# The order of matrix units in a Strassen MLP: one more unit of the first matmul ahead of a unit of the second, one fewer later

## The chip, the cores and the metric

The kernel runs on one NeuronCore of a Trainium2 chip. The metric is the device time of one execution in microseconds; the time given for a kernel is the median of several runs.

## The reference

Two decoder layers on 512 positions of width D = 1024, batch 1, in f32. Each layer modulates its norms with vectors from a condition `c`, mixes positions (layer 0 by pooling, layer 1 by a spatial gating unit), and then runs an MLP:

```python
for i in range(DEPTH):
    mod = c_act @ ada_w[i] + ada_b[i]
    sh1, sc1, g1, sh2, sc2, g2 = jnp.split(mod, 6, axis=-1)
    h = modulate(rmsnorm(x, norm_mix_g[i]), sh1, sc1)
    ...
    x = x + g1[:, None, :] * y
    h = modulate(rmsnorm(x, norm_mlp_g[i]), sh2, sc2)
    x = x + g2[:, None, :] * (jnp.square(jax.nn.relu(h @ mlp_w1[i])) @ mlp_w2[i])
return rmsnorm(x, final_g)
```

The MLP is 1024 to 4096 to 1024; it is most of the work, and the change concerns only it.

## The kernel before

**Precision.** TensorE has no full f32 product here: `split` (L170 to L178) writes a weight tile of 128 x 1024 as a rounded high part `wh` (ScalarE, L176) and a rest `wl` (VectorE, L177). `mm3` (L183 to L190) does every product as three matmuls: wl with the high part (L187), wh with the low part (L188), and wh with the high part (L190). The activations are cut likewise, `oh` on ScalarE (L638) and `ol` on VectorE (L639).

**Chunks and products.** `mlp` treats the 4096 hidden features in 4 chunks. M1 is the first matmul (into a chunk's hidden features), M2 the second (out of them). From chunk 1 on, M1 is done by the Strassen-Winograd scheme: each half (a or b) of a chunk is 7 products of block sums instead of 8. M2 of chunks 0 to 2 is done in the same way on the whole chunk. One product is a unit: an M1 unit (kind "s", written s1, s5, s6, ...) is 24 matmuls of 256 columns, an M2 unit (kind "p", written P1, P2, ...) 24 of 512. M1 of chunk c + 1 is interleaved with M2 of chunk c.

**Banks.** Products accumulate in PSUM where Winograd's sums allow: the M1 products 1, 6, 7, 4 pass through one bank of the tile `po` one after the other, 5 and 3 share another, and 2 has its own (`s_run`, L808ff). Between two products of one bank its content must be taken out: after 1, 6 and 5 by a ScalarE copy (L828), after 3 and 7 by a VectorE subtraction (L833, L835). After that come the squared ReLU's two ScalarE passes (L836, L667). M2's results are added into `y` by VectorE (L930), or copied by ScalarE (L933).

**Weights.** Some products need sums of weight blocks. These are built in place: by VectorE (L788), or by a DMA that accumulates into the tile, on GpSimd's queue. For M1 that is L783 on the tile `raw`: after the split of s6's weights, the block that makes s4's is added to them. For M2 it is L850 on the tile `bt` (from `w2`): P1's weights become P5's, these P6's, and these P4's, each as soon as the former has been split. Plain loads go over SyncE's queue.

**What sets the order.** The list `units` is written out by L975 to L988. PE runs it strictly as written. Ahead of each unit the loop at L1010 prepares further units (loads, weight sums, splits, cuts), at most 5 weight pairs ahead. On ScalarE, VectorE, GpSimd and SyncE the instructions are put in order by a scheduler when the kernel is built; at run time each engine works through its own queue in that order, so an instruction that waits holds up all behind it. The pools have 5 weight pairs `wh`/`wl`, 4 banks `po`, and 4 banks `pm` for M2.

The two tables of the changed line say how many M1 units come first (`lead`) and how many follow each M2 unit (`step`; M2's order is ORDER2 = 1, 2, 5, 6, 3, 7, 4). M1's order is ORDER = 1, 5, 6, 3, 7, 2, 4; the first half in layer 0's chunk 0 goes by ORDER2 with its 4 at the end. There, `early` is true. What is said below of "layer 0, chunk 0" is that of M2; its M1 units are those of chunk 1.

Of the kernel before, what the change touches and what calls it, by code (L numbers as in the profile page):

```python
# [81 lines left out]
def decoder_kernel(ctx: ExitStack, tc: tile.TileContext, xtok, vecs, rows, fgrow, ada0, adag, ada1, pool_w, w1s, w1, w1f, w1b, w2, w2e, w_v, w_u, w_o, wsT, lnp, bs, out):  # L82
# [561 lines left out]
    def mlp(i, first, extra, last, ending):  # L644
# [3 lines left out]
        with (  # L648
# [328 lines left out]
            for c in range(3):  # L977

                early = i == 0 and c == 0
                fs = [("s", (c + 1, j, m)) for j in range(2) for m in (ORDER2 if early and j == 0 else ORDER)]  # L980
                lead, step = (3, (0, 3, 2, 2, 2, 2, 0)) if early else (2, (1, 2, 3, 2, 2, 2, 0))
                units += fs[0:lead]
                fs = fs[lead:]
                for m, n in zip(ORDER2, step):
                    units.append(("p", (c, m)))
                    units += fs[0:n]
                    fs = fs[n:]
# [118 lines left out]
    ex += [(59, lambda: spread_cols(mods[0][:, c_g(1, 0) : c_g(1, 0) + KD], "gain0"))]  # L1106
    ex += [(n, modulation(q, get4)) for q, n in enumerate(COLUMNS) if q >= 19]
    mlp(0, first0, ex, gated, ending0)


# [6 lines left out]
    with (  # L1117
# [79 lines left out]
        for dh in range(2):  # L1197
            wo = blocks(w_o[dh])

            early = 6 if dh == 0 else KD  # L1200
# [60 lines left out]
    ex = [x for q in range(8) for x in modulation_late(48 + q, 8 + 5 * q, late_gb if q == 0 else get_gb)]  # L1261
    ex += [(58, lambda: spread_cols(mods[1][:, c_g(1, 0) : c_g(1, 0) + KD], "gain1"))]
    mlp(1, first1, ex, last1, lambda: None)


# [78 lines left out]
```

## Time and profile before

| | us |
|---|---|
| median of 3 runs | 855.63 (854.56 to 855.83) |
| the profiled execution | 853.81 |
| its span, first to last instruction | 852.1 |
| PE (TensorE) busy | 837.4 |
| DVE (VectorE) busy | 695.8 |
| ACT (ScalarE) busy | 490.9 |
| POOL (GpSimd) busy | 70.3 |

The mean granted clock of TensorE in the profiled execution is 0.993 of full speed. In the lines that follow, times in a timeline or in the chain of waits are microseconds from the start of the span. A row of a timeline has the start, the duration, the engine, the line, the operation, what it writes and reads, the count of equal operations in a row, and in brackets the idle time of the engine ahead of it with what ended it. Operations of one engine overlap a little in the profile, so what an operation costs its queue is read from one start to the next.

### The profile page before, as it was taken

The numbers are of one execution on the slowest core, as the hardware profiler recorded it, in microseconds if no ns is written. First come the engines' busy times: TensorE is split into PE (matmuls) and PEld (weight loads), VectorE is DVE, ScalarE is ACT, GpSimd is POOL, SyncE is SP. The second block draws the span as 40 slices with busy tenths as digits, with TensorE's granted clock in tenths as the row PEclk, the third lists the DMA queues.
The fourth block names the chain that finished last, engine by engine and source line by source line (L and its number), as shares of the span: only waits on it lengthen the run. The fifth ranks groups of instructions, "written<-read, shape, count | busy, mean of one in ns | idle before, by whom it ended". The sixth has DMA issues, their size and how long they took to land.

```text
span 852.1 us, 13021 instructions
## 1 busy us (share of the span) xinstructions
PE 837.4 (98%) x5068; PEld 744.6 (87%) x5068; DVE 695.8 (82%) x928; ACT 490.9 (58%) x728; POOL 70.3 (8%) x95
## 2 busy tenths in 40 slices
PE   9999999999999999999999999999999999999996
PEld 7778898998998998888888888999999999999885
DVE  6889798978997998867897865777788888987755
ACT  5286776765756567247233226666766666566521
POOL 3000011010101010000020001010101000111001
PEclk9999999999999999999999999999999999999998
DMA  8969998988888896724745636947888788777302
GB/s 349 418 234 323 357 216 217 288 212 236 211 282 195 274 237 205 272 98 173 256 166 176 218 123 224 320 94 202 208 238 221 207 222 241 182 168 243 125 25 99
DMA packets 44082, 186.53 MB, mean 219 GB/s; under 512 B 4955, under 2 KB 5107, under 8 KB 36726
## 3 DMA queue, kind: packets, MB, share of 16 engines
q1 hardware_dynamic: 35282, 137.72, 43.7%
q0 software_dynamic: 8304, 45.63, 26.7%
q10 hardware_dynamic: 436, 2.37, 0.8%
q8 instruction: 40, 0.66, 0.3%
q14 instruction: 20, 0.16, 0.1%
HBM read 179.39 MB, written 6.30 MB: 218 GB/s over the span
## 4 chain that ended last, share of the span: by engine, by line
PE 87%; DMA 6%; ACT 3%; DVE 2%; issue 1%; SPq 0%; POOLq 0%; POOL 0%; DVEq 0%; ACTq 0%
PE po L187 16%; PE po L188 16%; PE po L190 16%; PE pm L188 12%; PE pm L190 12%; PE pm L187 12%; DMA wh<-in_ada 2%; DMA bt<-in_w 2%; DMA wl<-in_ada 1%; DMA ada<-in_adag 1%; PE po L1182 1%; ACT sq L315 1%; PE px L1062 1%; ACT wh L176 0%; PE po L611 0%
## 5 line engine op out<-in xcount | busy, mean ns | idle before, releaser
L187 PE MATMUL po<-hb,wl 128*128 128x256 f32 (+2 forms) x633 | 187.9, 297 | 2.3 <-ACT g L828 2.1
L188 PE MATMUL po<-hb,wh 128*128 128x256 f32 (+1 forms) x632 | 187.2, 296 | 0.0
L190 PE MATMUL po<-hb,wh 128*128 128x256 f32 (+1 forms) x632 | 187.1, 296 | 0.0
L177 DVE TENSOR_TENSOR wl<-raw,wh 128x1024 fp32r<-128x1024 f32 (+1 forms) x128 | 152.8, 1198 | 39.4 <-ACT wh L176 36.8
L176 ACT ACTIVATE wh<-raw 128x1024 fp32r<-128x1024 f32 (+1 forms) x128 | 131.9, 1038 | 79.6 <-PE pm L190 26.7
L190 PE MATMUL pm<-wh,oh 128*128 128x512 f32 (+1 forms) x375 | 131.1, 367 | 0.0
L187 PE MATMUL pm<-wh,ol 128*128 128x512 f32 x336 | 131.0, 390 | 0.0
L188 PE MATMUL pm<-wl,oh 128*128 128x512 f32 x336 | 131.0, 390 | 0.0
L187 PEld LDWEIGHTS po<-hb,wl 128*128 128x128 f32 x633 | 119.6, 189 | 7.0 <-ACT g L828 2.3
L190 PEld LDWEIGHTS po<-hb,wh 128*128 128x128 f32 x632 | 119.5, 189 | 4.1
L188 PEld LDWEIGHTS po<-hb,wh 128*128 128x128 f32 x632 | 119.4, 189 | 3.9
L190 PEld LDWEIGHTS pm<-wh,oh 128*128 128x128 f32 x375 | 70.4, 188 | 14.7
L187 PE MATMUL po<-as,wl 128*128 128x256 f32 x288 | 79.9, 277 | 0.7 <-DVE wl L177 0.7
L188 PE MATMUL po<-as,wh 128*128 128x256 f32 x288 | 79.6, 277 | 0.0
L190 PE MATMUL po<-as,wh 128*128 128x256 f32 x288 | 79.6, 276 | 0.0
L177 DVE TENSOR_TENSOR wl<-bt,wh 128x1024 fp32r<-128x1024 f32 x48 | 58.4, 1222 | 23.5 <-ACT wh L176 23.5
L215 DVE SCALAR_TENSOR_TENSOR ada<-ada,cb 128x1024 f32<-128x1024 f32 x56 | 68.1, 1219 | 10.4 <-DMA ada<-in_ada 7.8
L187 PEld LDWEIGHTS pm<-wh,ol 128*128 128x128 f32 x336 | 63.1, 188 | 11.9
L188 PEld LDWEIGHTS pm<-wl,oh 128*128 128x128 f32 x336 | 63.1, 188 | 11.7
L176 ACT ACTIVATE wh<-bt 128x1024 fp32r<-128x1024 f32 x48 | 50.3, 1057 | 25.6 <-DMA bt<-in_w 15.9
L187 PEld LDWEIGHTS po<-as,wl 128*128 128x128 f32 x288 | 54.1, 188 | 0.9 <-ACT wh L176 0.9
L188 PEld LDWEIGHTS po<-as,wh 128*128 128x128 f32 x288 | 54.2, 188 | 0.0
(218 smaller groups left out, 1549.9 us busy)
## 6 DMA issues: line engine op xcount, KB each, us to landing
ada<-in_ada SPq DMA_DIRECT2D x72, 512.0 KB, 4.5
raw<-in_w1b SPq DMA_DIRECT2D x48, 512.0 KB, 5.5
b<-in_w SPq DMA_DIRECT2D x18, 1024.0 KB, 6.8
bt<-in_w POOLq DMA_DIRECT2D x18, 1024.0 KB, 8.0
raw<-in_w1b POOLq DMA_DIRECT2D x24, 512.0 KB, 5.7
raw<-in_w2e SPq DMA_DIRECT2D x16, 512.0 KB, 4.3
bt<-in_w SPq DMA_DIRECT2D x6, 1024.0 KB, 9.8
b<-in_w POOLq DMA_DIRECT2D x6, 1024.0 KB, 11.1
```

The source lines that it names most:

```text
L176: A.activation(h[:, c], r[:, c], AF.Copy)
L177: V.tensor_tensor(l[:, c], r[:, c], f32(h[:, c]), ALU.subtract)
L187: T.matmul(o[:, c], wl, mh[:, c], start=first and not c.start, stop=False, **kw)
L188: T.matmul(o, wh, ml, start=False, stop=False, **kw)
L190: T.matmul(o[:, c], wh, mh[:, c], start=False, stop=last and c.stop is None, **kw)
L215: V.scalar_tensor_tensor(r, r, 1.0, cb, ALU.mult, ALU.mult, accum_out=pmv[i, b][:, j : j + 1])
L315: A.activation(j, X(t)[:, c], AF.Square, scale=D**-0.5, accum_out=out)
L1062: T.transpose(px[:, 256 * q + P * r : 256 * q + P * r + P], xs[r][:, P * (k + q) : P * (k + q) + P], ident)
L1182: T.matmul(po[:, tok[t]], vt[t][:, ch, c0 : c0 + P], wb[:, 0, hd], start=True, stop=True)
```

## The change

```diff
                 fs = [("s", (c + 1, j, m)) for j in range(2) for m in (ORDER2 if early and j == 0 else ORDER)]
-                lead, step = (3, (0, 3, 2, 2, 2, 2, 0)) if early else (2, (1, 2, 3, 2, 2, 2, 0))
+                lead, step = (3, (0, 4, 2, 2, 2, 1, 0)) if early else (3, (1, 2, 2, 2, 2, 2, 0))
                 units += fs[0:lead]
                 fs = fs[lead:]
                 for m, n in zip(ORDER2, step):
                     units.append(("p", (c, m)))
                     units += fs[0:n]
                     fs = fs[n:]
```

In layer 0, chunk 0, four M1 units stand between P2 and P5 instead of three, and one instead of two between P7 and P4:

```
before  s1a s2a s5a P1 P2 s6a s3a s7a     P5 s4a s1b P6 s5b s6b P3 s3b s7b P7 s2b s4b P4
after   s1a s2a s5a P1 P2 s6a s3a s7a s4a P5 s1b s5b P6 s6b s3b P3 s7b s2b P7 s4b     P4
```

In the other five chunks three M1 units stand ahead of P1 instead of two, and two instead of three between P5 and P6:

```
before  s1a s5a     P1 s6a P2 s3a s7a P5 s2a s4a s1b P6 (the rest is equal)
after   s1a s5a s6a P1 s3a P2 s7a s2a P5 s4a s1b     P6
```

The amount of work of each kind is unchanged. Where instructions move, the queues show. PE first, at the end of s7a in layer 0, chunk 0 (`wh_1185` and `wl_1186` are s7a's weights, `wh_1228` is P5's first pair, `wh_1222` and `wl_1223` are s4a's in the changed kernel). Before:

```order
L188 MATMUL po_1045<-hb_96,wh_1185 128x256
L190 MATMUL po_1045<-hb_96,wh_1185 128x256
L187 MATMUL pm_1331<-wh_1228,ol_1225 128x512
L188 MATMUL pm_1331<-wl_1229,oh_1224 128x512
L190 MATMUL pm_1331<-wh_1228,oh_1224 128x512
```

After:

```order
L188 MATMUL po_1045<-hb_96,wh_1185 128x256
L190 MATMUL po_1045<-hb_96,wh_1185 128x256
L187 MATMUL po_1045<-hb_96,wl_1223 128x256
L188 MATMUL po_1045<-hb_96,wh_1222 128x256
L190 MATMUL po_1045<-hb_96,wh_1222 128x256
```

The bank `po_1045`, which s7a has just filled, is the bank of the next unit too; before, a unit of M2 with banks of its own stood between.

ACT at the same place, from the last split before P5's input cut on. `raw_955` and `raw_949` hold s3a's and s7a's weights, `oh_1224` (`oh_1255` after) is P5's input, `bt_1026` P5's weights, L828 takes s6a out of `po_1045`, `raw_941` is s4a's weights and `raw_1183` s1b's. Before:

```order
L176 ACTIVATE wh_1179<-raw_955 128x1024
L176 ACTIVATE wh_1185<-raw_949 128x1024
L638 ACTIVATE oh_1224<-s_1222 128x1024
L176 ACTIVATE wh_1228<-bt_1026 128x1024
L176 ACTIVATE wh_1232<-bt_1026 128x1024
L828 ACTIVATE g_1044<-po_1045 128x2x256
L176 ACTIVATE wh_1262<-raw_941 128x1024
L176 ACTIVATE wh_1295<-raw_1183 128x1024
```

After:

```order
L176 ACTIVATE wh_1179<-raw_955 128x1024
L176 ACTIVATE wh_1185<-raw_949 128x1024
L638 ACTIVATE oh_1255<-s_1253 128x1024
L176 ACTIVATE wh_1222<-raw_941 128x1024
L828 ACTIVATE g_1044<-po_1045 128x2x256
L176 ACTIVATE wh_1259<-bt_1026 128x1024
L176 ACTIVATE wh_1263<-bt_1026 128x1024
L176 ACTIVATE wh_1295<-raw_1183 128x1024
```

The split of s4a's weights has moved ahead of L828 and of P5's splits; P5's splits have moved behind L828.

DVE at the same place, from the low part of P5's input on; L835 takes s7a out of `po_1045`. Before:

```order
L639 TENSOR_TENSOR ol_1225<-s_1222,oh_1224 128x1024
L177 TENSOR_TENSOR wl_1229<-bt_1026,wh_1228 128x1024
L177 TENSOR_TENSOR wl_1233<-bt_1026,wh_1232 128x1024
L177 TENSOR_TENSOR wl_1263<-raw_941,wh_1262 128x1024
L833 TENSOR_TENSOR g_1044<-po_1116,g_1044 128x2x256
L177 TENSOR_TENSOR wl_1296<-raw_1183,wh_1295 128x1024
L215 SCALAR_TENSOR_TENSOR ada_1191,pmv_963<-ada_1191,cb_101 128x1024
L835 TENSOR_TENSOR g_1044<-g_1044,po_1045 128x2x256
```

After:

```order
L639 TENSOR_TENSOR ol_1256<-s_1253,oh_1255 128x1024
L177 TENSOR_TENSOR wl_1223<-raw_941,wh_1222 128x1024
L869 TENSOR_TENSOR s_1253<-s_1253,g_919 128x1024
L177 TENSOR_TENSOR wl_1260<-bt_1026,wh_1259 128x1024
L177 TENSOR_TENSOR wl_1264<-bt_1026,wh_1263 128x1024
L833 TENSOR_TENSOR g_1044<-po_1116,g_1044 128x2x256
L177 TENSOR_TENSOR wl_1296<-raw_1183,wh_1295 128x1024
L215 SCALAR_TENSOR_TENSOR ada_1191,pmv_963<-ada_1191,cb_101 128x1024
L835 TENSOR_TENSOR g_1044<-g_1044,po_1045 128x2x256
```

s4a's subtraction and L869 (a sum for P6's input, which stood behind L835) have moved ahead of P5's two subtractions; L835 is behind them all.

The last place is ACT at the head of layer 0, chunk 2. `raw_2312` holds the weights of s6a, `bt_2590` (`bt_2596` after) P1's, `oh_2672` (`oh_2703`) is the next M2 input, and L828 takes s1a out of `po_2612`. Before:

```order
L176 ACTIVATE wh_2596<-bt_2590 128x1024
L667 ACTIVATE g_2207<-g_2207 128x2x256
L176 ACTIVATE wh_2600<-bt_2590 128x1024
L638 ACTIVATE oh_2672<-g_2207 128x1024
L176 ACTIVATE wh_2606<-raw_2312 128x1024
L828 ACTIVATE g_2611<-po_2612 128x2x256
```

After:

```order
L667 ACTIVATE g_2207<-g_2207 128x2x256
L176 ACTIVATE wh_2564<-raw_2312 128x1024
L176 ACTIVATE wh_2602<-bt_2596 128x1024
L176 ACTIVATE wh_2606<-bt_2596 128x1024
L638 ACTIVATE oh_2703<-g_2207 128x1024
L828 ACTIVATE g_2611<-po_2612 128x2x256
```

The split of s6a's weights has moved ahead of P1's two.

## The prediction

> **What bounds the kernel now.** I read the page first, then the list of waits of PE, then the chain of waits in the stretch that the first wait lies in, and last the timelines of PE, ACT and DVE there. From the page:
>
> ```profile
> span 852.1 us, 13021 instructions
> PE 837.4 (98%) x5068; PEld 744.6 (87%) x5068; DVE 695.8 (82%) x928; ACT 490.9 (58%) x728; POOL 70.3 (8%) x95
> ```
>
> PE is busy 98% of the span, so only two things can move the time: idle gaps of PE, and stretches in which its granted clock is low. The diff changes no matmul, only their order. The list of PE's waits over the whole span has two that lie in the MLPs (the columns are the total, the count and the longest):
>
> ```profile
> PE po L187 <- ACT g L828: 2.1, 1, 2.1
> ...
> PE po L187 <- DVE wl L177: 0.9, 2, 0.7
> ```
>
> The first is the larger, and one wait. It lies in layer 0, chunk 0, ahead of product 7 of the first half of M1 (I write s7 for that unit, P5 for product 5 of M2). The chain of waits there:
>
> ```profile
> 111.65 15.97 DMA bt<-in_w
> 127.70 2.00 ACT wh L176 x2
> 129.71 0.49 ACT g L828
> ```
>
> The accumulating transfer that builds P5's weights took 15.97 us. ACT, which works in its queue's order, stood waiting for it, and behind the two splits stood the evacuation L828 of s6, whose bank s7 overwrites. PE's timeline and the windows cut at the 3.42 us steps in which the clock changes show what that cost:
>
> ```profile
> 127.87 0.28 PE L190 MATMUL po<-as,wh 128*128 128x256 f32 x1
> 130.25 0.38 PE L187 MATMUL po<-hb,wl 128*128 128x256 f32 x1 [2.10 <-ACT g L828]
> 134.69 0.39 PE L187 MATMUL pm<-wh,ol 128*128 128x512 f32 x1
> ...
> 127.11:130.53 3.42, 1.32 (x12) 1.12 (x11) 1.73 (x2) 2.49 (x3) 0.00 (x0) 1.00 1.05 280
> 130.53:133.95 3.42, 3.42 (x18) 3.42 (x18) 1.77 (x2) 1.85 (x2) 0.85 (x1) 0.50 1.03 322
> 134.69:140.15 5.46, 5.46 (x27) 4.55 (x26) 5.17 (x7) 2.27 (x4) 0.00 (x0) 1.00 0.99 260
> 140.15:142.89 2.74, 2.74 (x26) 2.74 (x25) 1.79 (x2) 2.74 (x5) 0.86 (x1) 1.00 0.82 211
> ```
>
> The columns of a window are its length, then busy time of PE, weight loads, DVE, ACT and POOL, the granted clock, the DMA share and GB/s. s7 should have begun at 127.98 (127.87 and a step of 0.11) and began at 130.25: 2.27 lost. PE was busy 1.32 of 3.42 us, and the next such window ran at clock 0.50. So s7 took 134.69 − 130.25 = 4.44 us, not the 2.74 of the undisturbed unit s4 (140.15 to 142.89): 1.70 more. P5 is the row of 5.46. Before, s7 and s4 stand with P5 between them, and the second half of M1 (s1b) starts at 142.89.
>
> **The change, term by term.** The new order puts s4 ahead of P5, and prepares it first. Two queues follow from that.
>
> *ACT.* Before, in order of time:
>
> ```profile
> 127.70 2.00 ACT L176 ACTIVATE wh<-bt 128x1024 fp32r<-128x1024 f32 x2 [5.00 <-DMA bt<-in_w]
> 129.62 0.58 ACT L828 ACTIVATE g<-po 128x512 f32<-128x512 f32 x1
> 131.72 1.06 ACT L176 ACTIVATE wh<-raw 128x1024 fp32r<-128x1024 f32 x1 [1.53 <-DMA raw<-in_w1b]
> 133.16 1.06 ACT L176 ACTIVATE wh<-raw 128x1024 fp32r<-128x1024 f32 x1 [0.38 <-DMA raw<-in_w1b]
> ...
> 122.46 0.86 POOL L783 DMA_DIRECT2D raw<-in_w1b  x1 [9.96 <-DVE wl L177]
> ...
> DMA to landing us min/median/max: 9.2/9.2/9.2
> ```
>
> After, the split of s4's weights (the row at 131.72) stands ahead of L828, and P5's two splits behind it. That split waits for the accumulating transfer issued by POOL at 122.46, which took 9.2 us and ends at 131.6. Neither POOL's nor SP's queue changes ahead of that, and all of M1 and M2 up to there is as before, so I keep 131.72. Two splits in a row advance the queue by (129.62 − 127.70) / 2 = 0.96 each. So L828 starts at 132.68 and ends at 133.26; s7 follows 0.05 later (129.62 + 0.58 = 130.20, then 130.25), at 133.31. P5's wait is gone, and a wait for another transfer, with the same victim, is 3.06 us longer.
>
> *DVE.* s4 accumulates in the bank of s7, so it must wait until DVE's L835 has taken s7 out. Before, the 5.46 us of P5 lay between. Now nothing does. DVE's queue before:
>
> ```profile
> 128.80 2.36 DVE L177 TENSOR_TENSOR wl<-bt,wh 128x1024 fp32r<-128x1024 f32 x2 [2.02 <-ACT wh L176]
> 132.81 1.23 DVE L177 TENSOR_TENSOR wl<-raw,wh 128x1024 fp32r<-128x1024 f32 x1 [1.65 <-ACT wh L176]
> 133.95 0.69 DVE L833 TENSOR_TENSOR g<-po,g 128x512 f32<-128x512 f32 x1
> 134.55 1.22 DVE L177 TENSOR_TENSOR wl<-raw,wh 128x1024 fp32r<-128x1024 f32 x1
> 135.69 1.22 DVE L215 SCALAR_TENSOR_TENSOR ada<-ada,cb 128x1024 f32<-128x1024 f32 x1
> 136.83 0.68 DVE L835 TENSOR_TENSOR g<-g,po 128x512 f32<-128x512 f32 x1
> 137.50 1.22 DVE L869 TENSOR_TENSOR s<-s,g 128x1024 f32<-128x1024 f32 x1
> ```
>
> A full operation advances the queue by 1.14 (132.81 to 133.95), a half one by 0.60 (133.95 to 134.55). After, the row at 132.81, which still starts at that time, is followed by L869, P5's two subtractions, L833, the next subtraction, L215, and only then L835: 132.81 + 5 × 1.14 + 0.60 + 1.14 = 140.25, with its end at 140.93. s4 starts at 140.98 with the same 0.05.
>
> *Clock.* The window to 130.53 holds even less matmul time than before, so the next one is at 0.50, and in that PE works 133.31 to 133.95 only (0.64 of 3.42, less than the 1.32 that brought the drop before). So I let the window to 137.36 run at 0.50 too. s7 does 4.05 / 2 = 2.03 of its 2.72 in it and ends at 138.05. PE then waits until 140.98. The window 137.36 to 140.78 holds 0.69 of matmul, again less than 1.32, so the next one, to 144.19, is half speed: s4 does 3.21 / 2 = 1.60 there, and the other 1.14 behind it, ending at 145.33. P5 has its weights since 137.4 and takes 5.46. The second half starts at 150.79, which was 142.89: **+7.9 us**. Without the last drop s4 ends at 143.72 and the lag is +6.3.
>
> The Trainium skill ("TensorE: Matmul & The Clock Gate", "Why this matters for your kernels") states that there should be no gap over about 3 us, because one window of idle halves the clock. Taken as a whole idle window, that would leave s4 at full speed, +6.3; here a gap of 2.27 us already brought clock 0.50, so the trace goes against it, and I stay with +7.9.
>
> *P6.* POOL's next transfer into P5's buffer waits for P5's last subtraction:
>
> ```profile
> 131.45 0.85 POOL L850 DMA_DIRECT2D bt<-in_w  x1 [8.13 <-DVE wl L177]
> ```
>
> Before, that came 0.3 us behind it (128.80 + 2.36). It moves to about 137.7; even with 16 us it would land by 154, while P6, two M1 units behind 150.79, starts at 156.2. Nothing.
>
> *The other chunks* get three M1 units (s1, s5, s6) ahead of P1 and one fewer ahead of P6. P1's transfer gains a unit, 2.7 us. In exchange s6 needs L828 of s1 one unit after s1, where P1 (5.46) lay between. PE's second wait is one that goes; layer 0, chunk 2:
>
> ```profile
> 271.07 0.40 PE L190 MATMUL pm<-wh,oh 128*128 128x256 f32 x2
> 272.18 0.36 PE L187 MATMUL po<-as,wl 128*128 128x256 f32 x1 [0.72 <-DVE wl L177]
> ...
> 262.51 1.06 ACT L176 ACTIVATE wh<-bt 128x1024 fp32r<-128x1024 f32 x1 [3.82 <-DMA bt<-in_w]
> 264.95 1.04 ACT L638 ACTIVATE oh<-g 128x1024 fp32r<-128x1024 f32 x1
> ```
>
> 271.07 and a step of 0.11 more for the second of the pair leaves 272.18 − 271.29 = 0.89 lost. After, that split and subtraction stand ahead of P1's, so the 0.89 goes; but L828 of s1 then stands behind P1's two splits and the cut of its input, which start at about 262.6: 262.6 + 3 × 0.96 + 0.58 = 266.1, where s6 would start one M1 unit and P1 (2.72 + 5.46) ahead of 271.29 + 2.72 = 274.0, at 265.8. About 0.4 is left: **−0.5**. The bounds are −0.9 (no wait left) and 0. In the other four heads I take 0, by hand reading of the order with the same durations; each could cost as much as this one did, 0.9.
>
> **Sum.** +7.9 − 0.5 = +7.4 on the profiled execution's 853.81 (its span of 852.1 and 1.7 around it): 861.2. The median shown, 855.63, lies 1.8 above it, so I forecast 863.0. PE has nothing later that could take the lag up: the other waits of its list lie before 120 us or are under half a microsecond.
>
> **Rivals.**
>
> *R1, the transfer is quicker.* All 24 such transfers have this row:
>
> ```profile
> raw<-in_w1b POOLq DMA_DIRECT2D x24, 512.0 KB, 5.7
> ```
>
> At 5.7 us it lands at 128.2, L828 ends at 129.8, s7 starts about then, and DVE's queue is free sooner. But the next subtraction waits for the transfer behind the ACT row at 133.16, so L835 still starts at 133.16 + 0.96 + 0.2 + 2 × 1.14 = 136.6 and s4 at 137.4. 3.6 us earlier than in my forecast: +4.3, net +3.8, or +2.2 without the second drop: 857.8 to 859.4. Against it: DMA is full there (shares of 1.03 and 1.05 above), and order and state up to it are as before. 0.12.
>
> *R2, faster: the extra unit covers P5's transfer.* If s4's transfer landed by 126.4, its split and L828 would be done at 127.98, and if L835 then stood early enough, neither wait would be left: −2.27 − 1.70 − 0.89 = −4.9, 850.8. It decides at 3.9 us from issue to landing, where the trace has 9.2. By the Trainium skill ("DMA: Bandwidth & Descriptors", "Anatomy of one DMA — SWDGE (gpsimd) path") a fixed 2.0 us and the bytes by 436 GB/s would give an estimate of 3.2 us, which is this case; the 9.2 and 15.97 measured here speak against it. 0.05.
>
> *R3, no change.* The waits come out shorter than R1 by one of its drops, or the chunk heads give back more: within 0.2% of 855.63 (1.7 us, about what a measurement of this kernel can tell from no change). 0.05.
>
> *R4, the chunk heads wait too.* Five heads now ask for L828 within one unit. At 0.9 each, with none gone in chunk 2, that is +4.5 on +7.9: 868. For it: ACT idles for M2 transfers in front of those evacuations. Against it: in the other heads the M2 transfer lands well before. 0.13.
>
> My forecast, with or without the last half-speed window (863.0 or 861.4), keeps 0.65.
>
> **How the numbers follow.** The forecast's own bounds are 861.0 (no wait left in chunk 2, no last drop) to 863.5. R1 reaches down to 857.8, and half of R4 up to 866. 858.4 to 866.0 leaves out R2, R3, the lower end of R1 and the upper half of R4, about 0.18. Faster by over 0.2%: R2, 0.05. Same: R3, 0.05. Slower: the rest, 0.90.
>
> **What would show it.** In the list of PE's waits after: L187 waiting for ACT's L828 for about 5.3 us (127.98 to 133.31), a new wait of L187 for DVE's L835 of about 2.9 us, and none for P5's weights. In the timelines: ACT's split ahead of L828 still ending its idle at 131.7; L835 at 140.2; clock 0.50 from 130.53 to 144.19, as far as PE works in it; s1b from 150.8. If s7 starts before 130 my price of the transfer is wrong; if L835 stands at 137 or sooner, the DVE sum is; if PE's waits at the chunk heads sum to over 1 us, R4 is at work.

## The result, and the profile after

The changed kernel takes 867.56 us (median of 4 runs, 866.64 to 867.99), the kernel before on the same chip 855.25 us (4 runs, 854.56 to 855.83): a ratio of 1.0143, 95% interval 1.0124 to 1.0161, or 12.3 us more. The forecast was 863.0, in a range up to 866.0: slower, as forecast, but by two thirds more. The profiled execution took 867.73 us. From its page:

```profile
span 865.6 us, 13010 instructions
PE 844.2 (98%) x5068; PEld 749.6 (87%) x5068; DVE 694.9 (80%) x928; ACT 490.0 (57%) x728; POOL 70.3 (8%) x95
```

The same work, in a span that is 13.5 us longer. The list of PE's waits, all that stand in its MLPs:

```profile
PE po L187 <- ACT g L828: 6.4, 2, 4.8
PE po L187 <- DVE g L835: 3.0, 1, 3.0
PE po L187 <- DVE wl L177: 1.3, 2, 1.1
...
PE pm L188 <- DVE wl L177: 0.5, 1, 0.5
PE pm L187 <- DVE ql L639: 0.4, 1, 0.4
```

Before there were one wait for L828 of 2.1 us and two for `wl` of 0.9 together. The wait of 4.8 for L828 and that of 3.0 for L835 are the two that the prediction put into chunk 0. Of the rest it had 0.4 us at the head of chunk 2, where the second wait for L828 (1.6) lies; it had neither the wait for `wl` of 1.1 nor the two small ones.

To see where they lie, the span is cut at the starts of units that have the same work done ahead of them in both kernels. In layer 0: from s1a of chunk 0 to s1b; of chunk 2, from s1a to s1b and from s1b to the plain M2 units of the last chunk (M2 without Strassen's sums, also 24 matmuls of 512 columns each); and the first of these. The windows of the kernel after:

```profile
103.98:152.24 48.26, 40.44 (x244) 37.20 (x243) 39.73 (x39) 31.05 (x41) 5.42 (x6) 0.89 0.80 208
...
269.64:307.06 37.42, 35.78 (x246) 32.85 (x244) 31.31 (x39) 20.50 (x27) 2.58 (x3) 1.00 0.85 241
307.06:349.49 42.43, 41.34 (x271) 37.44 (x269) 38.28 (x46) 29.59 (x42) 4.78 (x7) 1.00 0.70 207
349.49:356.33 6.84, 5.91 (x25) 4.27 (x24) 6.70 (x10) 3.77 (x7) 0.00 (x0) 1.00 0.59 194
```

The same stretches before:

```profile
103.44:142.89 39.45, 37.35 (x244) 34.40 (x243) 34.53 (x35) 28.30 (x38) 5.43 (x6) 0.96 0.92 243
260.38:296.84 36.46, 35.74 (x246) 32.83 (x244) 32.77 (x42) 22.80 (x30) 3.26 (x4) 1.00 0.83 232
296.84:337.92 41.08, 41.08 (x271) 37.35 (x269) 36.93 (x46) 28.89 (x42) 4.11 (x7) 1.00 0.77 219
337.92:343.36 5.44, 5.44 (x25) 4.50 (x24) 5.44 (x9) 2.25 (x4) 0.00 (x0) 1.00 0.65 216
```

The differences: chunk 0 +8.81, the head of chunk 2 +0.96, its second half +1.35, the first plain M2 unit +1.40. The stretches between these agree within 0.11, and so does chunk 1. Another 0.54 lies ahead of the MLP (103.98 against 103.44), the remaining 0.4 behind these stretches.

**Chunk 0, step by step.** PE's timeline after, at the place whose rows of before stand in the prediction, and then ACT's and DVE's:

```profile
133.46 0.56 PE L187 MATMUL po<-hb,wl 128*128 128x256 f32 x1 [4.78 <-ACT g L828]
141.11 0.58 PE L187 MATMUL po<-hb,wl 128*128 128x256 f32 x1 [3.04 <-DVE g L835]
```

```profile
131.86 1.06 ACT L176 ACTIVATE wh<-raw 128x1024 fp32r<-128x1024 f32 x1 [8.61 <-DMA raw<-in_w1b]
132.82 0.58 ACT L828 ACTIVATE g<-po 128x512 f32<-128x512 f32 x1
```

```profile
132.95 1.23 DVE L177 TENSOR_TENSOR wl<-raw,wh 128x1024 fp32r<-128x1024 f32 x1 [5.64 <-ACT wh L176]
...
140.37 0.69 DVE L835 TENSOR_TENSOR g<-g,po 128x512 f32<-128x512 f32 x1
```

Less the 0.54 by which all of it lies later: L828 at 132.28 (forecast 132.68), s7a at 132.92 (133.31), L835 at 139.83 (140.25), s4a at 140.57 (140.98). The two sums hold to half a microsecond. The clock differs. Cut at its own steps:

```profile
136.92:140.34 3.42, 1.16 (x10) 0.96 (x8) 3.42 (x4) 1.62 (x4) 0.85 (x1) 1.00 0.30 41
140.34:143.75 3.41, 2.64 (x12) 2.64 (x13) 3.36 (x7) 2.29 (x3) 0.86 (x1) 0.50 1.01 207
143.75:147.16 3.41, 3.41 (x16) 3.31 (x15) 2.06 (x2) 0.52 (x2) 0.00 (x0) 0.50 0.97 237
```

Half speed lasted two windows behind the second wait, to 147.16 and into P5, not one. That is why s1b came 0.9 us later than forecast (152.24 less 0.54 is 151.70, against 150.79). The rule of the Trainium skill that the prediction weighed ("TensorE: Matmul & The Clock Gate", "Why this matters for your kernels") warns of gaps over about 3 us, because one window of idle halves the clock. The second gap is 3.04 us, as that rule has it; but a whole idle window was not needed, for the window that held the gap had 1.16 us of matmul, as one with 1.32 was enough before.

**Chunk 2.** PE stands for 1.64 us for L828 at the head (s6a, at 276.90), and for 1.09 us for `wl` at s6b:

```profile
276.90 0.38 PE L187 MATMUL po<-as,wl 128*128 128x256 f32 x1 [1.64 <-ACT g L828]
...
319.23 0.36 PE L187 MATMUL po<-as,wl 128*128 128x256 f32 x1 [1.09 <-DVE wl L177]
```

The chain of waits that ends at s6b begins far ahead of it, at P6's weights:

```profile
297.01 9.15 DMA bt<-in_w
...
306.24 1.07 ACT wh L176
...
315.51 1.23 DVE raw L788
...
317.86 1.24 DVE wl L177
319.23 0.36 PE po L187
```

Between the first ACT row and the last of DVE, DVE has no pause above 1.2 us; it works through its queue, and two units behind P6 PE has caught up with it. P6 itself started on time (309.78, in order behind s1b). What was late is what stands behind its splits in the queues. The first rows of ACT's splits for this P6, before and then after:

```profile
293.63 2.01 ACT L176 ACTIVATE wh<-bt 128x1024 fp32r<-128x1024 f32 x2 [0.36 <-DMA bt<-in_w]
```

```profile
306.24 1.06 ACT L176 ACTIVATE wh<-bt 128x1024 fp32r<-128x1024 f32 x1 [4.13 <-DMA bt<-in_w]
```

ACT stood 4.1 us for this transfer, where it had stood 0.4. Before, the transfer was issued 14.3 us ahead of P6's start (285.30 and 299.56) and landed 6.0 ahead of it (8.2 us later); after, it was issued 12.8 ahead (297.01) and landed 3.6 ahead.

### The profile page after: what moved, and what is told of

It reads as the page before. It is cut to its first block, busy times and chain, and to the rows that moved or that the text cites. A ratio compares the mean times of both kernels' runs of the same rounds, so it can differ in the third digit from the quotient of the medians.

```text
span 865.6 us, 13010 instructions
## 1 busy us (share of the span) xinstructions
PE 844.2 (98%) x5068; PEld 749.6 (87%) x5068; DVE 694.9 (80%) x928; ACT 490.0 (57%) x728; POOL 70.3 (8%) x95
## 4 chain that ended last, share of the span: by engine, by line
PE 80%; DVE 8%; DMA 4%; issue 3%; ACT 3%; POOLq 0%; POOL 0%; DVEq 0%; ACTq 0%
PE po L187 14%; PE po L188 14%; PE po L190 14%; PE pm L187 10%; PE pm L188 10%; PE pm L190 10%; DVE wl L177 3%; DMA bt<-in_w 2%; PE po L479 2%; PE pg L431 1%; ACT wh L176 1%; DMA raw<-in_w1b 1%; PE pq L465 1%; PE po L1182 1%; DVE ada L215 1%
## 5 line engine op out<-in xcount | busy, mean ns | idle before, releaser
L188 PEld LDWEIGHTS pm<-wl,oh 128*128 128x128 f32 x336 | 63.2, 188 | 11.7
```

The source lines that it names most:

```text
L188: T.matmul(o, wh, ml, start=False, stop=False, **kw)
```

## The experiments

None of these kernels leaves work out. Times are medians; a difference is given with the ratio to the runs of the kernel before on the same chip, and its interval. That kernel's own median on these chips lay between 853.7 and 854.5. A run can differ by 1 to 2 us ahead of the MLP, so the stretches of the profile tell more than the totals. The next table has them for layer 0, in the order of time: chunk 0 (s1a to s1b), chunk 1 (the same), chunk 2 (the same), the second half of chunk 2 (s1b to the plain M2 units), the first plain M2 unit. Each is the difference of two starts in PE's timeline.

| kernel | chunk 0 | chunk 1 | chunk 2 | 2nd half | plain M2 |
|---|---|---|---|---|---|
| before | 39.45 | 35.61 | 36.46 | 41.08 | 5.44 |
| after | 48.26 | 35.50 | 37.42 | 42.43 | 6.84 |
| early_only | 45.57 | 35.50 | 35.50 | 41.08 | 5.44 |
| others_only | 36.41 | 37.60 | 37.57 | 42.31 | 6.85 |
| heads_only | 36.76 | 37.56 | 38.20 | 41.09 | 6.34 |
| p6_only | 37.38 | 37.03 | 37.89 | 43.60 | 6.88 |
| c2_only | 36.76 | 36.08 | 36.65 | 42.57 | 6.78 |
| layer1_only | 36.58 | 37.42 | 35.54 | 41.08 | 5.47 |
| s4_behind | 47.20 | 35.49 | 35.49 | 41.08 | 5.44 |
| l835_first | 46.09 | 35.50 | 35.49 | 41.08 | 5.51 |
| p5_behind3 | 36.90 | 37.04 | 35.79 | 41.08 | 5.44 |
| halves_others | 36.44 | 36.51 | 35.50 | 41.08 | 5.44 |
| halves_before | 37.39 | 35.50 | 36.49 | 41.09 | 5.44 |
| halves_after | 48.07 | 35.50 | 35.50 | 41.08 | 5.44 |
| halves_p5 | 37.01 | 35.49 | 35.49 | 41.08 | 5.44 |

The second half of chunk 1 is not in the table: it takes 40.94 to 41.02 in all profiles but others_only (41.31) and p6_only (42.70). Where the table of units is that of before, chunks 0 and 1 still differ between profiles: layer1_only, which runs all of layer 0 in the order of before, takes 2.9 us less in chunk 0 than the profile before and 1.8 more in chunk 1, where it has this wait ahead of P5:

```profile
PE pm L187 <- DVE y L930: 1.7, 1, 1.7
```

So a difference of 1 to 2 us in chunk 1, or of up to 3 in chunk 0, is not by itself a cost of an edit.

### Which part of the change costs what

early_only changes chunk 0 alone:

```diff
-lead, step = (3, (0, 3, 2, 2, 2, 2, 0)) if early else (2, (1, 2, 3, 2, 2, 2, 0))
+lead, step = (3, (0, 4, 2, 2, 2, 1, 0)) if early else (2, (1, 2, 3, 2, 2, 2, 0))
```

> Only the table of layer 0, chunk 0, is changed; the other five chunks are as before. Both theories hold the two waits in chunk 0 (s7a for L828, s4a for L835) and their half-speed windows for one cost of about 8.8 us, as the trace of the changed kernel has it there. Theory P6 (the unit taken from ahead of P6 in the other chunks costs the rest, by ACT's and DVE's queues): nothing else is late, 864.1 us, +8.8 on before; PE waits at the head of chunk 2 as before (0.7 to 0.9 us). Theory heads (the evacuation L828 in the five chunk heads costs the rest): the same 864.1. If chunk 0 alone brings all of the 12.3 us, both fall.

Measured: 862.42 us, ratio 1.0099 (1.0073 to 1.0125). In the profile all of it lies in chunk 0. What the expectation had wrong is the head of chunk 2, which takes 35.50 here, less than before: the old wait of 0.9 is gone. PE comes 6.8 us later there than in the profile before, so ACT and DVE may have caught up; this is not shown, for layer1_only, where PE comes 0.5 us earlier than before, has no such wait either (35.54).

others_only changes the other five alone:

```diff
+lead, step = (3, (0, 3, 2, 2, 2, 2, 0)) if early else (3, (1, 2, 2, 2, 2, 2, 0))
```

> Only the table of the other five chunks is changed; layer 0, chunk 0 is as before. By the prediction on record (-0.5 for these chunks): 854.8 us. Theory P6 and theory heads: about +3.5 (0.9 more at the head of layer 0, chunk 2; 1.2 at its s6b; 1.5 at the plain M2 units behind it), 858.8 us; the two differ in the next two runs.

Measured: 858.62 us, ratio 1.0053 (1.0034 to 1.0073). The prediction's −0.5 falls. There is a wait that neither kernel has shown, 1.9 us at the head of chunk 1 (37.60); the kernel after has none there (35.50), behind its long waits in chunk 0. layer1_only loses as much in that chunk with the table of before (37.42), at another place, so this wait need not be a cost on top. The two largest entries of the list of PE's waits of this kernel's layer 0:

```profile
PE po L187 <- ACT g L828: 3.4, 2, 1.7
PE po L187 <- DVE wl L177: 1.0, 1, 1.0
```

layer1_only gives the changed table to layer 1 alone:

```diff
+lead, step = (3, (0, 3, 2, 2, 2, 2, 0)) if early else (3, (1, 2, 2, 2, 2, 2, 0)) if i else (2, (1, 2, 3, 2, 2, 2, 0))
```

> Only layer 1's three chunks have the changed kernel's table. By both theories layer 1's queues have slack (no wait of PE in its MLP in either profile): no change from before, within 0.2%.

Measured: 854.45 us, ratio 0.9999 (0.9984 to 1.0014). As expected: the cost is layer 0's.

### Heads, or P6?

heads_only keeps the three units ahead of P1, gives P6 its three back, and takes the unit from between P6 and P3 instead:

```diff
+lead, step = (3, (0, 3, 2, 2, 2, 2, 0)) if early else (3, (1, 2, 3, 1, 2, 2, 0))
```

> The other five chunks have three M1 units ahead of P1 as in the changed kernel, but three between P5 and P6 as before (the unit is taken from between P6 and P3 instead). Chunk 0 as before. Theory heads: the evacuation behind P1's splits costs what it cost in the changed kernel, +3.5, 858.8 us. Theory P6: DVE runs 1.4 us less late, so s6 of chunk 2 waits 0.4 us instead of 0.9 before, and nothing waits behind it: 854.8 us (-0.5).

Measured: 857.77 us, ratio 1.0046 (1.0028 to 1.0064). Of my theory P6, a part holds: the second half of chunk 2 is at 41.09, the wait at s6b is gone. The rest falls: the heads of chunks 1 and 2 wait longer than in the kernel after, not less, and the first plain M2 unit still loses 0.9 of the 1.4 us (6.34). PE's list of waits from 180 to 300 us has nothing else:

```profile
PE po L187 <- ACT g L828: 4.2, 2, 2.4
```

p6_only does the reverse, two units ahead of P1 as before, and two between P5 and P6:

```diff
+lead, step = (3, (0, 3, 2, 2, 2, 2, 0)) if early else (2, (1, 3, 2, 2, 2, 2, 0))
```

> The other five chunks have two M1 units ahead of P1 as before, but two between P5 and P6 as in the changed kernel (the unit goes between P2 and P5 instead). Chunk 0 as before. Theory heads: no change, 855.3 us. Theory P6: DVE is 1.4 us late from P6 of chunk 1 on, so s6 of chunk 2 waits 0.9 + 1.4 us; s6b of chunk 2 waits 1.2 us and the plain M2 units 1.5: +4.1, 859.4 us.

Measured: 862.31 us, ratio 1.0088 (1.0063 to 1.0114). The theory of the heads alone falls as well: with the heads as before, the cost is larger still, and it lies where theory P6 puts it (chunk 2, its second half, the plain units), with 1.4 in chunk 1 and 1.8 in its second half besides. This run and the one before it each move the unit to or from a third place as well, so neither separates the heads from P6 cleanly.

c2_only gives the changed table to layer 0's chunk 2 alone:

```diff
+lead, step = (3, (0, 3, 2, 2, 2, 2, 0)) if early else (3, (1, 2, 2, 2, 2, 2, 0)) if (i, c) == (0, 2) else (2, (1, 2, 3, 2, 2, 2, 0))
```

> Only layer 0's chunk 2 has the changed kernel's table; chunk 0 and chunk 1 are as before, so DVE comes to chunk 2 no later than it did before. Theory queue (the head of chunk 2 waits for L828 by 0.4 us plus what DVE is behind PE there, and DVE got behind at P6 of chunk 1): 0.4 us at the head instead of 0.9, 1.2 at s6b and 1.4 at the plain M2 units: +2.1 on before. Theory head (three units ahead of P1 cost a wait of 1.8 us there by themselves): 1.8 at the head, +3.5 on before.

Measured: 856.40 us, ratio 1.0031 (1.0015 to 1.0048). The head waits 0.9 us, between the 0.4 and the 1.8 expected; s6b and the plain units wait as they do after. ACT at this head, c2_only and then the kernel after:

```profile
260.31 1.06 ACT L176 ACTIVATE wh<-raw 128x1024 fp32r<-128x1024 f32 x1 [2.42 <-DVE raw L788]
261.68 2.01 ACT L176 ACTIVATE wh<-bt 128x1024 fp32r<-128x1024 f32 x2 [0.32 <-DMA bt<-in_w]
...
264.55 0.57 ACT L828 ACTIVATE g<-po 128x512 f32<-128x512 f32 x1
```

```profile
272.46 1.07 ACT L176 ACTIVATE wh<-raw 128x1024 fp32r<-128x1024 f32 x1 [2.42 <-DVE raw L788]
...
276.27 0.58 ACT L828 ACTIVATE g<-po 128x512 f32<-128x512 f32 x1
```

Measured from the start of s1a (258.80 and 269.64), the first split starts after 1.51 us in c2_only and after 2.82 in the kernel after. So there ACT and DVE are 1.3 us further behind PE when chunk 2 begins; and in c2_only, where they are not, ACT's only pause behind the first split is 0.3 us for P1's transfer. The head's wait is the queues' lateness, brought along from chunk 1, as much as its own order. In heads_only, where P6 has its three units, the first split comes later still, 3.61 us after s1a (264.04 and 260.43): it is not P6's splits alone that make the queues late there.

halves_others tests what makes the queues late. The table is that of others_only. Each transfer that adds M2 weights goes out in two halves, the first as soon as the first half of the old weights has been split:

```diff
-b_add(wb, c, *CHAIN[nxt])
+for q in range(2):
+    G.dma_start(wb[:, 2 * q : 2 * q + 2], w2[i, c, CHAIN[nxt][0], CHAIN[nxt][1]][:, 2 * q : 2 * q + 2], accum_op=ALU.add)
```

> As others_only, but each accumulating transfer of M2 weights (1 MB, issued when both halves of the former weights are split) is issued as two of 512 KB, the first as soon as the first half is split. The table is unchanged, P6's weights land sooner. Theory P6 transfer (ACT's and DVE's queues stand at P6's splits until that transfer lands, and s6b of chunk 2 and the plain M2 units pay for it): the stretch from s1b of chunk 2 to the plain M2 units falls from 42.3 to 41.1 to 41.5 us and their first part from 6.85 to under 6.4; 1 to 2 us less than others_only. Theory order (the queues' order is late by itself, whatever the transfer): both stretches as in others_only.

Measured: 853.20 us, ratio 0.9993 (0.9978 to 1.0009), where others_only had 1.0053. The order of ACT's and DVE's instructions is that of others_only but for a handful of rows. The waits at s6b and at the plain units are gone, the head of chunk 2 waits no more, and that of chunk 1 0.8 instead of 1.9 us. So it was M2's accumulating transfers; and since heads_only, with P6's three units back, had no wait at s6b either, for that one it was P6's. Which of them makes the head of chunk 2 late stays open. One rival is left: GpSimd's queue also carries the transfers of L783, and with the halves these go out earlier too. The chain of waits at s6b has M2's transfer and none of these, but no run changes one without the other.

halves_after makes the same edit in the changed kernel:

> The changed kernel, both tables, with the halved transfers. Theory P6 transfer: what the other chunks cost goes (no wait at the head of chunk 2, none at s6b, none at the plain M2 units), what chunk 0 costs stays, since L828 and L835 wait there for s4a's transfer and DVE's queue: 45.5 to 48.5 us from s1a to s1b of chunk 0 and 7 to 9 us over before. If the other chunks' cost follows from chunk 0's waits in some way that others_only does not show, over 10.

Measured: 861.50 us, ratio 1.0072 (1.0050 to 1.0094), 6.2 us over before by the ratio, a little under the 7 to 9 expected. Outside chunk 0, layer 0's MLP runs without a wait. The two parts measured alone, 1.0099 (early_only) and 1.0053 (others_only), add up to the 1.0143 of both, within their intervals.

### What makes chunk 0 wait

s4_behind has early_only's table, holds s4a's preparation back by one unit, and orders L828 ahead of the split of s4a's weights:

```diff
+        if after is not None:
+            A.activation(h[:, 0:1], after, AF.Copy)
...
-                w = split(wb)
+                w = split(wb, after=g[1, 0][:, 2, 0:1] if i == 0 and u == (1, 0, 4) else None)
```

> As early_only, but a one-column ScalarE copy that reads what L828 writes stands ahead of the split of s4a's weights, so that ACT runs L828 before it stands waiting for their transfer. DVE's queue is as in early_only: L835 behind s4a's subtraction, P5's two, L833, the next one and L215. Theory DVE queue (s4a's start is set by DVE's row of L835 alone, the ACT wait lies under it): PE waits once instead of twice, s4a still starts about 140, and the time stays within 1.5 us of early_only's. Theory ACT (the wait behind s4a's split is a cost of its own, as the prediction adds it up): 3 to 4 us less than early_only.

Measured: 862.11 us, ratio 1.0104 (1.0081 to 1.0127), the time of early_only. L828 (here L830) stands at 125.72, PE does not wait for it, and PE's longest wait is now a single one, for L835 (here L837):

```profile
PE po L189 <- DVE g L837: 8.8, 1, 8.8
```

```profile
125.72 0.60 ACT L830 ACTIVATE g<-po 128x512 f32<-128x512 f32 x1 [2.74 <-PE po L192]
```

```profile
132.91 1.23 DVE L179 TENSOR_TENSOR wl<-raw,wh 128x1024 fp32r<-128x1024 f32 x1 [4.61 <-ACT wh L178]
...
139.20 0.68 DVE L837 TENSOR_TENSOR g<-g,po 128x512 f32<-128x512 f32 x1
```

s4a starts 36.23 us after s1a, where it started after 37.27 in early_only; the half-speed windows, three for two, take that back. So the wait for L828, 4.9 us in early_only's list, is worth nothing by itself. DVE's queue behind s4a's transfer sets the start of s4a, with or without it.

l835_first leaves that wait and moves the other: with early_only's table, P5 is prepared behind s7a, with its splits ordered behind L835 by the same one-column copy:

```diff
-w = [split(wb[...]) for q in range(2)]
+w = [split(wb[...], after=g[1, 0][:, 3, 256:257] if i == 0 and u == (0, 5) else None) for q in range(2)]
```

> As early_only, but P5 is prepared after s7a, and a one-column copy that reads what L835 writes stands ahead of P5's two splits, so that DVE takes s7a out of its bank before it subtracts for P5. ACT's queue ahead of L828 is as in early_only. Theory DVE queue: L835 starts as soon as s7a is done, PE's wait for it (2.2 to 3.0 us) falls under 1 us, and the time is 2 to 3 us less than early_only's. Theory ACT: the second wait is only a follow-on of the first; s4a starts no earlier, the time is early_only's.

Measured: 866.73 us, ratio 1.0157 (1.0139 to 1.0175). As for the cause, theory DVE queue holds: the wait for L835 falls to 0.8 us, and s4a starts 1.4 us earlier, 35.88 us after s1a. As for the time, the run is a miss: P5's weights are now late, PE waits 1.2 us for them behind s4a, and the stretch from s1b of chunk 0 to chunk 1 takes 46.78 instead of 40.96. Most of that lies far behind, at P4, which waits for `y` and brings another half-speed window (189.56 to 192.97):

```profile
PE pm L189 <- DVE y L932: 3.2, 1, 3.2
```

What makes that wait, no run shows.

### Can the wait of the kernel before be had?

p5_behind3 has the tables of before, with P5's splits ordered behind L828 of s6a and s4a's behind L835 of s7a, each prepared later:

```diff
-w = [split(wb[...]) for q in range(2)]
+w = [split(wb[...], after=g[1, 0][:, 2, 0:1] if i == 0 and u == (0, 5) else None) for q in range(2)]
...
-w = split(wb)
+w = split(wb, after=g[1, 0][:, 3, 256:257] if i == 0 and u == (1, 0, 4) else None)
```

> All tables as before. P5 is prepared one unit later, and one-column copies keep its splits behind L828 of s6a, and the split of s4a's weights behind L835 of s7a. If the wait of the kernel before is only ACT's queue order: s7a starts right behind s3a, at most 0.8 us are lost ahead of s4a, and the stretch from s1a of chunk 0 to s1b takes 35.5 to 36.2 us, where it took 39.4 in the profile before and 36.4 to 37.4 in the three other profiles with the same table: 1 to 3 us less than before. If DMA sets it (the transfers of P5 and s4a are just late), no change.

Measured: 855.53 us, ratio 1.0024 (1.0010 to 1.0039), slower if anything. The wait ahead of s7a is gone, and two others stand for it in layer 0's MLP. The second lies ahead of P5 of chunk 1, where layer1_only has it without this edit:

```profile
PE pm L189 <- DVE y L932: 1.3, 1, 1.3
PE po L189 <- DVE wl L179: 1.1, 1, 1.1
```

halves_before has the tables of before with the halved transfers, the edit of halves_others:

> The kernel before with the same halved transfers. Theory P6 transfer: nothing in the other chunks waits for them with three units ahead of P6; in chunk 0 the wait ahead of s7a (P5's transfer of 16 us) shrinks or goes, so 0 to 1.5 us less than before. Against: two issues on GpSimd's queue instead of one, each about 0.9 us, with s4a's transfer behind them.

Measured: 852.37 us, ratio 0.9993 (0.9976 to 1.0009): no change, and the wait ahead of s7a stays, at 1.5 us. halves_p5 has both edits, that of p5_behind3 and that of halves_others, with the tables of before:

> All tables as before, with the halved transfers and with P5's splits behind L828 and s4a's split behind L835 (halves_before and p5_behind3 together). If the two gains add: no wait ahead of s7a (1.7 us there in halves_before) and no wait behind chunk 0 in chunk 1 (1.4 us there in p5_behind3): 1 to 2 us less than before. If the one wait only moves to the next transfer, as in p5_behind3: within 0.2% of before.

Measured: 851.88 us, ratio 0.9965 (0.9941 to 0.9989), the one version that beats both kernels. Its interval overlaps that of halves_before, so what p5_behind3's edit adds to the halved transfers is not shown. In layer 0's MLP one wait is left, 1.3 us ahead of s4a.

## Why the prediction was right or wrong

*Direction and chunk 0: right, 0.9 too small.* Both waits came, at the forecast places and within half a microsecond, for the reasons given. The mis-sized term is the clock: one half-speed window was counted behind the second wait, two came (48.26 − 39.45 = 8.8 for 7.9). The prediction carried the clock's steps over from the profile before; in the kernel after they lie 0.4 us earlier (126.68 for 127.11) and the work 0.5 later. How many windows a wait hits was luck. With the same table in chunk 0, early_only had none behind its second wait and took 45.57, 6.1 over before, close to the +6.3 that the prediction gives for that case:

```profile
136.50:139.91 3.41, 2.77 (x14) 2.48 (x12) 3.41 (x5) 2.37 (x5) 0.85 (x1) 0.50 0.36 73
139.91:143.32 3.41, 1.87 (x16) 1.88 (x17) 3.41 (x6) 1.86 (x3) 0.43 (x1) 1.00 0.88 171
```

The wait for L828 is in the list but not in the price: s4a's start was computed from DVE's queue alone, and s4_behind shows that only this counts.

*The step that failed: the other chunks.* The prediction has −0.5 at the head of chunk 2 and no term at all behind it. They cost +3.7 (0.96 + 1.35 + 1.40). ("In the other four heads I take 0" held in the kernel after: chunk 1 takes 35.50, and layer 1 has no wait.) That "one fewer ahead of P6" could cost anything in those chunks was not priced at all; the P6 step ("Nothing") looked at chunk 0, and there only at whether P6 itself starts in time. It does, in chunk 2 too. But ACT and DVE stand at its splits until the transfer lands (4.1 us on ACT), and PE pays later: 1.35 at s6b, and a part of the 1.40 at the plain M2 unit. heads_only, with P6's three units back, has the one at 0 and the other still at 0.9 (it also takes a unit from behind P6). The wait at the head of chunk 2 was forecast at 0.4 and came out at 1.8, because the queues come late to that chunk (2.82 us after s1a, 1.51 in c2_only). halves_others keeps the table and makes M2's transfers land sooner, and all three go; which transfer makes the head late stays open.

*Rivals.* R1, R2 and R3 did not come. s4a's transfer took 8.8 us (123.00 to 131.77 by the chain of waits) for 9.2 before, far from R2's 3.9. The estimate of 3.2 us that R2 works out from the Trainium skill ("DMA: Bandwidth & Descriptors", "Anatomy of one DMA — SWDGE (gpsimd) path") does not hold here either. R4 had the right place for one of the three waits, the head of chunk 2, and by the prediction's own sign (over 1 us at the heads, 1.64 came) it was at work there. It would have needed waits in layer 1 and in chunk 1, and there are none in the kernel after. That its 868 lies beside the measured 867.56 is luck: it priced five heads, and one head and two places behind P6 came.

*The baseline.* The prediction took the 4 us ahead of and in s7a as a fixed property of the kernel before. Five other profiles with the same table in chunk 0 and the same transfers (others_only, heads_only, p6_only, c2_only, layer1_only) lose 0.9 to 1.9 us there (36.41 to 37.38, against 35.5 for the same units without a wait, as in chunk 1), since their gap in PE did not bring half speed. So up to 4.9 us to be gained, R2's sum, was less from the start, and the +8.81 goes with the profile that it is taken against: beside layer1_only, chunk 0 of the kernel after costs 11.7, and chunk 1 gives 1.9 back. The wait of 0.89 at the head of chunk 2, from which the −0.5 was taken, is not fixed either: layer1_only has none with the same order.

## What to carry to other kernels

A transfer whose consumer starts on time can still be late: ask what stands behind the first instruction that waits for it in each engine's queue, and when PE needs that. When a unit that covers a wait is moved from one place to another, price the place that loses it as carefully as the one that gains it. Two waits in a row for different engines need not add: remove the later one's cause in thought first, and see what start it alone would set.

## What the runs showed of the hardware

- A gap halved the clock of the next 3.42 us window when the window that held it had 1.16 (after) or 1.32 us (before) of matmul; no whole idle window was needed. A window with 1.87 us (early_only, 139.91 to 143.32) brought no drop, nor did heads_only's wait of 2.4 us at the head of chunk 2.
- Full speed did not return after a window with 2.64 of 3.41 us of matmul (140.34 to 143.75, after); it did after one with 2.77 us (early_only, 136.50 to 139.91).
- An accumulating transfer of 1 MB took 8.2 us before and 9.2 after at the same place; as two of 512 KB, 5.4 and 7.0 us (halves_others), the first issued 2.3 us ahead of the second.
